# Between two layers of a decoder trunk: four output tiles on all tokens, the next chunks split earlier, squares summed in narrow groups

## The chip, the cores and the metric

The kernel runs on one NeuronCore of a Trainium2 chip. The metric is the device time of one execution in microseconds (us). Three runs of the kernel before took 1275.55, 1278.9 and 1277.45 us; their median is 1277.45.

## The reference

Two layers work on 512 tokens of 1024 features in float32. Each layer has a token mixer and a gated feed-forward part, and each of these four sub-layers starts with a norm that is scaled and shifted by a condition:

```
h = rms_norm(x, norm_mix[i]) * (1.0 + sc1) + sh1
mix = stick_breaking_attention(h, ...) if i % 2 == 0 else dsa_attention(h, ...)   # both end in  o @ w_out
x = x + g1 * mix
h = rms_norm(x, norm_ffn[i]) * (1.0 + sc2) + sh2
x = x + g2 * conv_ffn(h, ...)                                                     # ends in  (silu(gate) * val) @ w_down
```

where `rms_norm(x, g)` is `x * rsqrt(mean(x * x) + 1e-6) * g`, the mean over the 1024 features of a token.

## The kernel before

Everything lies transposed: features on the 128 partitions, tokens along the free side. `x` is eight tiles of 128 features x 512 tokens, and stays on the chip.

**Products.** A float32 product is made of three matmuls in a rounded float format (`mm3`, L247): high part of the weights times high part of the activations, low times high, high times low. A weight chunk is 128 x 1024 numbers (512 KB). `chunk_raw` (L175) loads it into one of six buffers in turn (`raws`); ScalarE copies it into its high part (`split_hi`, L208), VectorE subtracts to get the low part (`split_lo`, L216). High and low parts have four buffers each (`splits`), also taken in turn, so a split waits until the matmuls of the chunk four places earlier are done. `split_order` lists all chunks in their order of use, `pos` is the next one to split, and `fetch` issues loads, one chunk ahead of the split. All loads go through SyncE's queue (SP) in order; each waits only until the buffer that it fills has been read.

**Order of the work.** The order on each engine is the order of the program; every engine works through its own instructions strictly in that order and waits on semaphores for the others.

**Boundaries.** `boundary` (L376) joins a sub-layer that ends in an output projection to the next one, which starts with a norm and projections. It is called three times: at the end of the first attention (at about 241 us), of the first feed-forward part (609 us) and of the second attention (882 us). The very end of the kernel has a function of its own (`final_proj`, L476). In a boundary the last four weight chunks (`last`) give eight output tiles of 128 features. Before the change each is made in two halves of 256 tokens, `halves[0]` and `halves[1]`, each with 4 x 3 matmuls into a PSUM tile (`pt_l`). The steps of one tile are:

- `add_to_x` (L359, VectorE) adds the tile, times a gate, to `x`;
- `square` (L285, ScalarE) squares the new `x` into `sqt`;
- for the first half, `square_add` (L293, VectorE) adds the squares of tiles 0 to 6 into `sqa`;
- `sum_squares` (L298, TensorE) sums over the partitions by a float32 matmul with a matrix of ones: two of them for the first half, eight (one for each tile) for the second.

Then `norm_seed` (L315, ScalarE) takes a reciprocal square root, `norm_newton` (L321 to L323, VectorE) refines it, and `norm_ops` makes h, feature tile by feature tile: `u` (L330, VectorE), the high part of h (L333, ScalarE), its low part (L339, VectorE). The norm of the first half runs beside the output tiles of the second half, all of its steps ahead of the next projections. The next projections (`pt_first`) run first on the first half, four of them, and then, in `second_half`, on the second half. The four chunks that they need (`first`) are split during the second half's output tiles (two) and at the start of the next projections (two). ScalarE loads the function table of the reciprocal square root (`warm`, L374) after output tile 4.

PSUM has eight banks; a tile of the ring "z" or "tr" (two banks each) is free again when `add_to_x` has read it.

**Around it.** In the first attention `out_steps` (L827) runs the projection of the first half of the heads as filler, and `release` behind each of its four chunks splits the next chunk. In the second attention `uvc` (value weights) uses the buffers of the squares, which are idle then.

## Time and profile before

| | |
|---|---|
| median of three runs | 1277.45 us |
| profiled execution | 1276.47 us |
| its span (first to last instruction) | 1274.7 us |
| TensorE busy | 1263.3 us, 99% |
| VectorE busy | 926.8 us, 73% |
| ScalarE busy | 585.7 us, 46% |
| granted TensorE clock | 1.00 of full speed in all slices |

A page of the profile comes from one execution. In it PE is TensorE's matmuls, PEld its weight loads (which overlap the matmuls), DVE is VectorE, ACT ScalarE, POOL GpSimd, SP SyncE. Matmuls are pipelined: the duration of one holds more than its share of the engine, so the distance from one start to the next is what it costs. The same holds, less strongly, for VectorE and ScalarE.

### The profile page before, as it was taken

Reading aid. Unit: us, or ns where it says so; the run is one execution under the profiler, and the core shown is the slowest. Engines: PE = TensorE matmul, PEld = TensorE weight load, DVE = VectorE, ACT = ScalarE, POOL = GpSimd, SP = SyncE. Lnnn points to the kernel's source line nnn. Section 1 sums busy time; section 2 is a strip of 40 time slices with the busy share of each in tenths; the row PEclk is TensorE's granted clock in tenths of the full one; section 3 lists DMA queues with packets and bytes.
Section 4 is the critical chain, followed back from the end, with each engine's and each line's share of the span. In section 5 each row is a group of like instructions: output and inputs, shape, how many; then the busy total and the mean of one; then the engine's idle time right before and its main releaser. Section 6 shows DMA issues by size and latency. Waiting matters only on the chain.

```text
span 1274.7 us, 17853 instructions
## 1 busy us (share of the span) xinstructions
PE 1263.3 (99%) x6800; PEld 1055.8 (83%) x6800; DVE 926.8 (73%) x1587; ACT 585.7 (46%) x1041; POOL 60.5 (5%) x171
## 2 busy tenths in 40 slices
PE   8999999999999999999999999999999999999998
PEld 6888787898888888888987777888988888888887
DVE  5889998778777877885768878887866456456653
ACT  5477666454323323442445446655554334234430
POOL 0000000000000000000002350110000000000000
PEclk9999999999999999999999999999999999999999
DMA  9644444424575575655222222123232432423221
GB/s 369 216 137 133 136 130 135 130 67 122 197 254 185 179 242 193 188 182 159 85 67 67 84 75 74 52 83 115 68 88 69 125 95 73 127 85 99 75 91 67
DMA packets 49605, 163.15 MB, mean 128 GB/s; under 512 B 5696, under 2 KB 6720, under 8 KB 49520
## 3 DMA queue, kind: packets, MB, share of 16 engines
q1 hardware_dynamic: 49088, 161.23, 40.2%
q8 instruction: 53, 0.87, 0.3%
q10 hardware_dynamic: 432, 0.79, 0.2%
q14 instruction: 32, 0.26, 0.1%
HBM read 159.86 MB, written 2.14 MB: 127 GB/s over the span
## 4 chain that ended last, share of the span: by engine, by line
PE 93%; DVE 4%; DMA 1%; ACT 1%; issue 1%; SPq 0%; DVEq 0%
PE pt_u L248 11%; PE pt_u L249 11%; PE pt_u L250 11%; PE pt_d L248 5%; PE pt_d L249 5%; PE pt_d L250 5%; PE pt_l L249 2%; PE pt_l L250 2%; PE pt_l L248 2%; PE pt_first L249 2%; PE pt_first L248 2%; PE pt_first L250 2%; PE pt_q L248 2%; PE pt_q L250 2%; PE pt_q L249 2%; PE pt_qk L248 1%
## 5 line engine op out<-in xcount | busy, mean ns | idle before, releaser
L208 ACT ACTIVATE whi<-raw 128x1024 fp32r<-128x1024 f32 (+1 forms) x206 | 205.2, 1003 | 123.7 <-PE pt_d L250 95.5
L248 PE MATMUL pt_u<-hhi,whi 128*128 128x512 f32 x640 | 249.2, 389 | 0.0
L249 PE MATMUL pt_u<-hhi,wlo 128*128 128x512 f32 x640 | 249.0, 389 | 0.0
L250 PE MATMUL pt_u<-hlo,whi 128*128 128x512 f32 x640 | 249.0, 389 | 0.0
L216 DVE TENSOR_TENSOR wlo<-raw,whi 128x1024 fp32r<-128x1024 f32 (+1 forms) x194 | 223.5, 1154 | 11.6 <-ACT whi L208 10.6
L995 ACT ACTIVATE y<-pt_u,sm 128x512 f32<-128x512 f32 x80 | 62.2, 777 | 188.3 <-PE pt_u L250 188.3
L248 PEld LDWEIGHTS pt_u<-hhi,whi 128*128 128x128 f32 x640 | 120.1, 188 | 26.0 <-issue 1.1
L250 PEld LDWEIGHTS pt_u<-hlo,whi 128*128 128x128 f32 x640 | 120.1, 188 | 25.1
L249 PEld LDWEIGHTS pt_u<-hhi,wlo 128*128 128x128 f32 x640 | 120.1, 188 | 24.6
L996 DVE SCALAR_TENSOR_TENSOR y<-pt_u,sm,y 128x511 f32<-128x511 f32 x80 | 59.9, 748 | 97.1 <-ACT y L995 96.9
L248 PE MATMUL pt_d<-acthi,whi 128*128 128x512 f32 x288 | 112.0, 389 | 0.0
L249 PE MATMUL pt_d<-acthi,wlo 128*128 128x512 f32 x288 | 112.0, 389 | 0.0
L250 PE MATMUL pt_d<-actlo,whi 128*128 128x512 f32 x288 | 112.0, 389 | 0.0
L257 DVE SCALAR_TENSOR_TENSOR raw<-raw,cond 128x1024 f32<-128x1024 f32 x88 | 106.5, 1216 | 3.8 <-DMA raw<-wst 2.7
L359 DVE SCALAR_TENSOR_TENSOR x<-pt_d,mod,x 128x512 f32<-128x512 f32 x48 | 36.0, 749 | 72.8 <-PE pt_d L250 72.8
L232 ACT ACTIVATE acthi<-y 128x512 fp32r<-128x512 f32 x44 | 27.8, 632 | 105.3 <-DVE y L1014 105.3
L248 PE MATMUL pt_first<-hhi,whi 128*128 128x256 f32 (+1 forms) x224 | 68.5, 306 | 0.0
L249 PE MATMUL pt_first<-hhi,wlo 128*128 128x256 f32 (+1 forms) x224 | 67.1, 300 | 0.8 <-DVE wlo L216 0.8
L250 PE MATMUL pt_first<-hlo,whi 128*128 128x256 f32 (+1 forms) x224 | 66.9, 299 | 0.0
L250 PEld LDWEIGHTS pt_d<-actlo,whi 128*128 128x128 f32 x288 | 54.1, 188 | 11.3
L248 PEld LDWEIGHTS pt_d<-acthi,whi 128*128 128x128 f32 x288 | 54.1, 188 | 11.2
L249 PEld LDWEIGHTS pt_d<-acthi,wlo 128*128 128x128 f32 x288 | 54.1, 188 | 11.1
(253 smaller groups left out, 2594.8 us busy)
## 6 DMA issues: line engine op xcount, KB each, us to landing
raw<-wst SPq DMA_DIRECT2D x250, 512.0 KB, 3.7
raw<-wst SPq DMA_DIRECT2D x48, 384.0 KB, 3.1
th<-rb SPq DMA_DIRECT2D x16, 256.0 KB, 3.2
ada<-wst SPq DMA_DIRECT2D x4, 512.0 KB, 6.8
outT<-x SPq DMA_DIRECT2D x7, 256.0 KB, 2.0
x<-xT SPq DMA_DIRECT2D x5, 256.0 KB, 6.3
x<-xT ACTq DMA_DIRECT2D x3, 256.0 KB, 3.8
cond<-crow SPq DMA_DIRECT2D x1, 512.0 KB, 9.4
```

The lines of the kernel that those rows point to most:

```text
L208: act.activation(hi[:, :n], raw[:, :n], AF.Copy)
L216: engine.tensor_sub(lo[:, :n], raw[:, :n], hi[:, :n].bitcast(F32))
L232: act.activation(hi, src, AF.Copy)
L248: pe.matmul(out, lhsT=whi, rhs=ahi, start=start, stop=False)
L249: pe.matmul(out, lhsT=wlo, rhs=ahi, start=False, stop=False)
L250: pe.matmul(out, lhsT=whi, rhs=alo, start=False, stop=stop)
L257: dve.scalar_tensor_tensor(raw, raw, 1.0, cond, op0=OP.mult, op1=OP.mult, accum_out=dst)
L359: dve.scalar_tensor_tensor(x[f][:, c], pt, mod[l][:, g * KT + f:g * KT + f + 1], x[f][:, c], op0=OP.mult, op1=OP.add)
L995: act.activation(y, pt, AF.Identity, scale=cw[2], bias=sm[:, b + S_CB + c:b + S_CB + c + 1])
L996: dve.scalar_tensor_tensor(y[:, 1:], pt[:, :S - 1], cw[1], y[:, 1:], op0=OP.mult, op1=OP.add)
```

## The change

The first four output tiles of a boundary are made on all 512 tokens at once, the other four in halves as before. Their squares are also taken on all tokens, and `square_add` sums tiles 0 to 3 for both halves (tile 0 is squared straight into `sqa`). For the second half there remain five tiles of squares: the sum of tiles 0 to 3, and tiles 4 to 7. The first four of these five go through `group_squares`: four matmuls with 32 columns of the ones matrix, each writing its own 32 partitions of one PSUM tile; `copy_groups` (ScalarE) copies that tile, and two full matmuls then sum the copy and tile 7. This happens between the k steps of the next projections.

The last two of the four chunks of the output projection are split at the start of the boundary into spare buffers (`spare_tile`): attention buffers that are idle by then, or a pair of their own in the feed-forward part. For that, `release` falls away behind the last two chunks in `out_steps`. The table is loaded right after these splits. The four chunks of the next projections are split beside tiles 0 to 3. The norm steps of the first half are spread: five of its ten steps come ahead of the next projections, the others between their k steps. `norm_newton`'s temporary shares the buffers of `u`, and the value weights come in two loads instead of four.

```diff
+    whole = slice(0, S)
+
+    def square(f, c):
+        if f == 0:
+            sqs["acc"] = npool.tile([P, S], F32, name="sqa")
+            act.activation(sqs["acc"], x[f], AF.Square)
+            return None
+        if f < 4 or f % 2 == 0:
+            sqs["t"] = npool.tile([P, S], F32, name="sqt", bufs=2)
+        t = sqs["t"][:, :] if f < 4 else sqs["t"][:, halves[f % 2]]
+        act.activation(t, x[f][:, c], AF.Square)
         return t
 
-    def square_add(f, t):
-        if f == 0:
-            a = sqs["acc"] = npool.tile([P, H2], F32, name="sqa")
-            dve.tensor_copy(a, t)
-        else:
-            dve.tensor_add(sqs["acc"], sqs["acc"], t)
-
-    def sum_squares(t, start, stop):
-        if start:
-            sqs["pt"] = ptile([P, H2], "pt_norm", "z")
-        pe.matmul(sqs["pt"], lhsT=ones_mean, rhs=t, start=start, stop=stop)
+    def square_add(t, c):
+        if t is not None:
+            dve.tensor_add(sqs["acc"][:, c], sqs["acc"][:, c], t)
+
+    def sum_squares(tiles):
+        sqs["pt"] = ptile([P, H2], "pt_norm", "z")
+        for i, t in enumerate(tiles):
+            pe.matmul(sqs["pt"], lhsT=ones_mean, rhs=t, start=i == 0, stop=i == len(tiles) - 1)
+
+    def group_squares(tiles):
+        sqs["q"] = ptile([P, H2], "pt_sq", "x")
+        for i, t in enumerate(tiles):
+            pe.matmul(sqs["q"][32 * i:32 * i + 32], lhsT=ones_mean[:, :32], rhs=t, start=True, stop=True)
+
+    def copy_groups():
+
+        g = sqs["acc"][:, halves[0]]
+        act.activation(g, sqs["q"], AF.Copy, scale=D / 32)
+        return g
 
...
-        t = npool.tile([P, H2], F32, name="nt")
+        t = npool.tile([P, H2], F32, name="nt", tag="u", bufs=4)
...
-    def boundary(last, O, l, gate, nxt, first):
-
+    def boundary(last, O, l, gate, nxt, first, spare_tile):
 
         cks = [chunk(k, 0) for k in last[:2]]
-        unsplit = lambda: pos["i"] <= order.index(last[3])
         nl, gcol, sh, sc = nxt
         new_h()
         norm_scale(nl, gcol, sc)
-        while unsplit():
-            split_hi()
-            split_lo()
+        for i in range(2):
+            split_hi(lambda name, i=i: spare_tile(i, name))
+            split_lo(lambda name, i=i: spare_tile(i, name))
         cks += [chunk(k, 0) for k in last[2:]]
         fetch(pos["i"] + 1)
+        warm(AF.Abs_reciprocal_sqrt)
 
         begun = {}
 
-        def out_steps(hf, m, ks):
-            c = halves[hf]
+        def out_steps(c, m, ks):
             whi, wlo = cks[m // 2]
             if m not in begun:
-                begun[m] = ptile([P, H2], "pt_l", "tr" if hf or m % 2 == 0 else "z")
+                begun[m] = ptile([P, c.stop - c.start], "pt_l", "z" if m % 2 else "tr")
             for k in ks:
                 w = k * 256 + (m % 2) * P
                 mm3(begun[m], whi[:, w:w + P], wlo[:, w:w + P], O[k][0][:, c], O[k][1][:, c], k == 0, k == 3)
 
-        def out_tile(hf, m):
-
-            if hf or m > 2:
-                out_steps(hf, m, range(4))
-            elif m == 0:
-                for ks in (range(3), range(3, 4)):
-                    for i in range(3):
-                        out_steps(hf, i, ks)
-            add_to_x(l, gate, m, begun.pop(m), halves[hf])
-            return square(m, hf)
+        def out_done(c, m):
+            add_to_x(l, gate, m, begun.pop(m), c)
+            return square(m, c)
 
         prev = None
         for m in range(KT):
-            t = out_tile(0, m)
-            if prev is not None:
-                square_add(m - 1, prev)
+            c = whole if m < 4 else halves[0]
+            if m == 0:
+                for ks in (range(3), range(3, 4)):
+                    for i in range(2):
+                        out_steps(c, i, ks)
+            elif m > 1:
+                out_steps(c, m, range(4))
+            split_lo()
+            if m < 4:
+                split_hi()
+            t = out_done(c, m)
+            square_add(prev, whole if m < 5 else halves[0])
             prev = t
+        ops0 = norm_ops(nl, sh, 0)
+        group = [sqs["acc"][:, halves[1]]]
+        for m in range(4, KT):
+            c = halves[1]
             if m == 4:
-                warm(AF.Abs_reciprocal_sqrt)
-        ops0 = norm_ops(nl, sh, 0)
-        pend = []
-        for m in range(KT):
-            if m == 1:
-                sum_squares(sqs["acc"], True, False)
-                sum_squares(prev, False, True)
+                out_steps(c, m, range(3))
+                sum_squares([sqs["acc"][:, halves[0]], prev])
                 norm_seed(0)
-            if m >= 3:
-                sum_squares(pend[m - 3], m == 3, False)
-            pend.append(out_tile(1, m))
-            if m == 1:
+                out_steps(c, m, range(3, 4))
                 norm_newton(0)
-            if m in (2, 4):
-                split_hi()
-            if m in (3, 5):
-                split_lo()
-            for _ in range((0, 0, 1, 1, 2, 1, 2, 2)[m]):
-                next(ops0, None)
-        for m in range(KT - 3, KT - 1):
-            sum_squares(pend[m], False, False)
-        for _ in ops0:
-            pass
-        pts = [ptile([P, S], "pt_first", "mm" if i < 3 else "x") for i in range(4)]
+                next(ops0)
+            else:
+                out_steps(c, m, range(4))
+            if m == KT - 1:
+                next(ops0)
+            group.append(out_done(c, m))
+            if m < KT - 1:
+                next(ops0)
+        pts = [ptile([P, S], "pt_first", "mm") for i in range(3)]
         cs = [chunk(k, 0) for k in first[:2]]
-        split_hi()
         hs, c = hcur["h"], halves[0]
         for k in range(KT):
             for i in range(2):
                 w = slice(k * P, (k + 1) * P)
                 mm3(pts[i][:, c], cs[i][0][:, w], cs[i][1][:, w], hs[k][0][:, c], hs[k][1][:, c], k == 0, k == KT - 1)
-            if k == 1:
-                sum_squares(pend[KT - 1], False, True)
+            if k == 0:
+                group_squares(group[:4])
+                quarters = copy_groups()
+            if k == 2:
+                sum_squares([quarters, group[4]])
                 norm_seed(1)
-                split_lo()
+            next(ops0, None)
+            if k == 4:
                 norm_newton(1)
-                split_hi()
         ops1 = norm_ops(nl, sh, 1)
         for i in range(2, 4):
             for _ in range(2):
                 next(ops1, None)
             cs.append(chunk(first[i], 0))
+            if i == 3:
+                pts.append(ptile([P, S], "pt_first", "x"))
             project(pts[i][:, c], cs[i], hs, c)
         for _ in ops1:
             pass
...
-                    release()
+                    if mp < 2:
+                        release()
 
...
+                             lambda i, name: ap.tile([P, LW], F32R, name=name, tag=("at", "a")[i])[:, :D])
...
-                                [("kw",), ("qi", 0), ("qi", 1), ("qi", 2)]), man
+                                [("kw",), ("qi", 0), ("qi", 1), ("qi", 2)],
+                                lambda i, name: fp.tile([P, D], F32R, name=name, tag="spare" + name, bufs=2)), man
...
-                uvc = [npool.tile([P, H2], F32, name="uvc", tag="sqt" if i < 3 else "sqa", bufs=3 if i < 3 else 1) for i in range(4)]
-                for i in range(4):
-                    nc.sync.dma_start(uvc[i], wst[CH["uv",], :, i * H2:(i + 1) * H2])
+                uvc = [npool.tile([P, S], F32, name="uvc", tag="sqt", bufs=2) for i in range(2)]
+                for i in range(2):
+                    nc.sync.dma_start(uvc[i], wst[CH["uv",], :, i * S:(i + 1) * S])
...
-                first = boundary([("do", 1, m) for m in range(4)], O[4:], l, 2, (l, S_NF, 3, 4), up_first(l))
+                first = boundary([("do", 1, m) for m in range(4)], O[4:], l, 2, (l, S_NF, 3, 4), up_first(l),
+                                 lambda i, name: ap.tile([P, LW], F32R, name=name, tag=("L", "pT")[i], bufs=2)[:, :D])
```

## Rows read from the trace of the kernel before

**Rows 1.** The page: the span, the busy time of each engine, the engines' shares of the chain that ended last, and the loads of weight chunks (count, size, median us from issue to landing).
```profile
span 1274.7 us, 17853 instructions
PE 1263.3 (99%) x6800; PEld 1055.8 (83%) x6800; DVE 926.8 (73%) x1587; ACT 585.7 (46%) x1041; POOL 60.5 (5%) x171
...
PE 93%; DVE 4%; DMA 1%; ACT 1%; issue 1%; SPq 0%; DVEq 0%
...
raw<-wst SPq DMA_DIRECT2D x250, 512.0 KB, 3.7
```

**Rows 2.** Busy time by stage: the sum over the first boundary from its first output matmul at 241.15 to 279.90 us (taken in three stretches; the means are over these), and the start of the third boundary. Columns of the second row: from:to, length, then busy us and instructions of each engine, granted clock of TensorE, share of the DMA engines, GB/s.
```profile
sum 38.75, PE 38.75 PEld 38.22 DVE 30.64 ACT 21.23 POOL 0.00; mean PE 12.92 PEld 12.74 DVE 10.21 ACT 7.08 POOL 0.00
...
882.20:895.30 13.10, 12.15 (x101) 11.95 (x100) 10.10 (x21) 6.80 (x12) 0.00 (x0) 1.00 0.37 120
```

**Rows 3.** The chain that ended last, in order of time (start, us, what): in the first boundary the first and the last of 107 output matmuls of 256 columns in a row, the two sums behind them and one later sum; and the first and the last of 14 matmuls of 512 columns in a feed-forward part.
```profile
241.53 0.12 PE pt_l L249
...
254.25 0.12 PE pt_l L250
254.37 0.86 PE pt_norm L298 x4
...
258.09 0.43 PE pt_norm L298 x2
...
399.94 0.23 PE pt_u L250
...
402.89 0.23 PE pt_u L248
```

**Rows 4.** TensorE's matmuls in order of time (start, us, instruction) around a group of narrow sums in the second attention: four matmuls of 32 output partitions and 512 columns, each in two passes; one matmul between 706.33 and 707.19 is left out.
```profile
705.54 0.39 PE L250 MATMUL pt_q<-hlo,whi 128*128 128x512 f32 x1
705.86 0.63 PE L1117 MATMUL ssg<-q2g,ones_mean 128*32 128x512 f32 x3
705.88 0.62 PE L1117 MATMUL ssg<-q,ones_mean 128*32 128x512 f32 x1
706.31 0.60 PE L1117 MATMUL ssg<-q2g,ones_mean 128*32 128x512 f32 x3
706.33 0.59 PE L1117 MATMUL ssg<-q,ones_mean 128*32 128x512 f32 x1
...
707.19 0.39 PE L249 MATMUL pt_q<-hhi,wlo 128*128 128x512 f32 x1
```

**Rows 5.** The start of the third boundary in order of time, all engines; in brackets the idle time of the engine before the instruction and what ended it.
```profile
883.14 0.63 ACT L1483 ACTIVATE ohi<-bs 128x512 fp32r<-128x512 f32 x1 [1.59 <-DVE bs L1480]
883.81 0.69 DVE L1487 TENSOR_TENSOR olo<-bs,ohi 128x512 fp32r<-128x512 f32 x1 [0.70 <-ACT ohi L1483]
884.42 1.22 DVE L216 TENSOR_TENSOR wlo<-raw,whi 128x1024 fp32r<-128x1024 f32 x1
884.46 0.28 PE L248 MATMUL pt_l<-ohi,whi 128*128 128x256 f32 x1
885.69 0.39 PE L249 MATMUL pt_l<-ohi,wlo 128*128 128x256 f32 x1 [0.95 <-DVE wlo L216]
885.91 0.28 PE L250 MATMUL pt_l<-olo,whi 128*128 128x256 f32 x1
```

**Rows 6.** VectorE and ScalarE in order of time, each line the start and the length of one instruction: an add of 512 columns and the low part behind it (second boundary); then, in the first boundary, a squares' add of 256 columns, the table load, the seed, the three steps behind it and what follows them, a u and a low part of h, a high part of a chunk, a low part of a chunk and what follows it.
```profile
604.89 0.75 DVE L359 SCALAR_TENSOR_TENSOR x<-pt_d,mod,x 128x512 f32<-128x512 f32 x1 [2.20 <-PE pt_d L250]
605.55 1.22 DVE L216 TENSOR_TENSOR wlo<-raw,whi 128x1024 fp32r<-128x1024 f32 x1
...
253.37 0.42 DVE L293 TENSOR_TENSOR sqa<-sqa,sqt 128x256 f32<-128x256 f32 x1
...
249.66 1.28 ACT L374 ACT_TABLE_LOAD   x1
255.31 0.46 ACT L315 ACTIVATE ln<-pt_norm,ecols 128x256 f32<-128x256 f32 x1
257.10 0.41 DVE L321 TENSOR_TENSOR nt<-ln 128x256 f32<-128x256 f32 x1
...
258.35 0.48 DVE L359 SCALAR_TENSOR_TENSOR x<-pt_l,mod,x 128x256 f32<-128x256 f32 x1
262.30 0.47 DVE L330 SCALAR_TENSOR_TENSOR u<-ln,sfac,x 128x256 f32<-128x256 f32 x1
262.70 0.48 DVE L339 SCALAR_TENSOR_TENSOR hlo<-u,mod,hhi 128x256 fp32r<-128x256 f32 x1
262.75 1.04 ACT L208 ACTIVATE whi<-raw 128x1024 fp32r<-128x1024 f32 x1
264.28 1.21 DVE L216 TENSOR_TENSOR wlo<-raw,whi 128x1024 fp32r<-128x1024 f32 x1
265.41 0.47 DVE L330 SCALAR_TENSOR_TENSOR u<-ln,sfac,x 128x256 f32<-128x256 f32 x1
```

**Rows 7.** The loads at the first boundary: two low parts on VectorE (start, length), SyncE's queue of loads (the first of five starts at 235.73, the last ends 26.22 later, most of it waiting), and the loads issued from 230 to 245 us (count, size, median us from issue to landing).
```profile
234.49 1.21 DVE L216 TENSOR_TENSOR wlo<-raw,whi 128x1024 fp32r<-128x1024 f32 x1
242.86 1.22 DVE L216 TENSOR_TENSOR wlo<-raw,whi 128x1024 fp32r<-128x1024 f32 x1 [0.25 <-ACT whi L208]
235.73 26.22 SPq L177 DMA_DIRECT2D raw<-wst  x5
raw<-wst SPq DMA_DIRECT2D x5, 512.0 KB, 4.4
```

More of the change, by code (lines that the diff above doesn't have):

```diff
@@ L281, in kernel_body @@
     sqs = {}
-    def square(f, hf):
-        t = npool.tile([P, H2], F32, name="sqt", bufs=3)
-        act.activation(t, x[f][:, halves[hf]], AF.Square)
-        return t
-    def square_add(f, t):
-        if f == 0:
-            a = sqs["acc"] = npool.tile([P, H2], F32, name="sqa")
-            dve.tensor_copy(a, t)
-        else:
-            dve.tensor_add(sqs["acc"], sqs["acc"], t)
-    def sum_squares(t, start, stop):
-        if start:
-            sqs["pt"] = ptile([P, H2], "pt_norm", "z")
-        pe.matmul(sqs["pt"], lhsT=ones_mean, rhs=t, start=start, stop=stop)
+    whole = slice(0, S)
[8 more added lines that the diff above has]
+        act.activation(t, x[f][:, c], AF.Square)
+        return t
+    def square_add(t, c):
[13 more added lines that the diff above has]
+        return g
     hcur = {}
@@ L490, in done @@
             nc.sync.dma_start(outT[m][:, c], x[m][:, c])
-        whole = slice(0, S)
         for m in range(2):
@@ L977, in stick_layer @@
             first = boundary([("o", 1, m) for m in range(4)], [O[4 + k] for k in range(4)], l, 2,
-                             (l, S_NF, 3, 4), up_first(l))
+                             (l, S_NF, 3, 4), up_first(l),
+                             lambda i, name: ap.tile([P, LW], F32R, name=name, tag=("at", "a")[i])[:, :D])
         return first, man
@@ L1443, in pair_values @@
                         pe.matmul(pv[:, k * P:(k + 1) * P], lhsT=latf[:, k * P:(k + 1) * P],
-                                  rhs=uvc[h // 4][:, h % 4 * 64:h % 4 * 64 + P], start=True, stop=True)
+                                  rhs=uvc[h // 8][:, h % 8 * 64:h % 8 * 64 + P], start=True, stop=True)
                     vals[h] = [npool.tile([P, H2], F32, name="vals", tag="u", bufs=4) for _ in range(2)]
```

## The prediction, made before the changed kernel was run

> **What bounds the kernel now.** I read the page first, then the stages around the three boundaries, then single instructions. The reader is to see on the page that TensorE is busy 99% of the span at the full granted clock, and that it makes up 93% of the chain that ended last [rows 1]. So time goes only where TensorE gets less work or where one of its few gaps closes. The table of stages shows no gap in the first boundary: TensorE is busy for all of the 38.75 us, while VectorE has 30.64 us of work and ScalarE 21.23 [rows 2]. The third boundary has one: 12.15 us of work in 13.10 [rows 2]. The change must therefore be judged by TensorE's work first, and then by whether VectorE and ScalarE still deliver in time.
>
> **Part 1: four tiles on all tokens.** In the chain, the 256-column output matmuls run from 241.53 to the start of the squares at 254.37, 107 of them, so 0.1200 us each [rows 3]. The 512-column ones go from 399.94 to 402.89 in 13 steps, 0.2269 us each [rows 3]. One wide one thus saves 2 x 0.1200 - 0.2269 = 0.0131 us. Tiles 0 to 3 hold 4 x 12 = 48 such pairs in a boundary: 0.63 us, and 1.9 us in three boundaries.
>
> **Part 2: the sums of squares.** Before, a boundary has two of them for the first half of the tokens and eight for the second. The chain gives 0.86 us for two and 0.43 for one [rows 3], so ten cost 4.30 us. After it, two full ones for the first half stay (0.86), then four narrow ones that write 32 partitions each, then two full ones (0.86). The trace has the narrow form with 512 columns: from the start of the matmul ahead of it (705.54) to the second one behind it (707.19) are 1.65 us, of which two wide matmuls take 0.45; the group costs 1.20 [rows 4]. Its two passes start 0.45 us apart, side by side over all four (705.86 to 705.88, then 706.31 to 706.33), so the columns account for some 0.85 and the rest, 0.34, is paid around it. With 256 columns I estimate 0.43 + 0.34 = 0.77 us. From both sides: 0.43 (nothing around it) and 4 x 0.43 = 1.72 (no overlap). I take 0.77, since the row is the same form. A boundary then pays 0.86 + 0.77 + 0.86 = 2.49, saves 1.81, and three save 5.4 us. The Trainium skill, "TensorEngine Tiling (Array Packing)", section "Tiling Modes", speaks against the narrow form: a change of tiling mode drains the engine. The 0.34 us of the row agree with it. The same page, section "Overview", gives up to four times the speed for outputs of at most 32; by that alone the group would cost 0.43 and the sum would be 1.0 us lower.
>
> **Part 3: the gap at the third boundary.** TensorE starts a matmul at 884.46 and the next at 885.69, released by a low part, and the one after that follows at 0.22 instead of 0.12: 1.11 + 0.10 = 1.2 us lost [rows 5]. It is tile 2, which needs the second chunk's low part; VectorE began that only at 884.42, behind the last head's. With two tiles on all tokens ahead, TensorE has 18 x 0.2269 = 4.1 us for k = 0 to 2 and 1.4 for k = 3, so tile 2 starts near 887.7, when that low part (done 885.55) has been there for 2 us. The k = 3 operand, begun at 883.81 and 0.69 long [rows 5], is asked for at 886.4. The gap goes, and I see none that takes its place: -1.2 us.
>
> **Part 4: what moves on VectorE and ScalarE.** The four splits of the next chunks come into the first part, one to each wide tile. VectorE's prices, start to start: 0.66 for an add of 512 columns, 1.13 for a low part [rows 6]; for the squares' add of 512 columns, which the trace lacks, 0.42 to 0.69, by its 256-column form below and by a subtraction of 512 columns above (0.69 long, the next 0.61 after it) [rows 5, 6]; I take 0.61. A tile costs 0.66 + 0.61 + 1.13 = 2.40 us of VectorE against 12 x 0.2269 = 2.72 of TensorE. ScalarE needs 1.04 for a high part and, by a copy of 512 columns, some 0.63 for a square [rows 5, 6]. Both fit. The last low part falls beside tile 4, where TensorE takes 1.44 and VectorE 2.14; tiles 5 to 7 bring 0.40 + 0.42 against 1.44 each and take that up. The table load of 1.28 us [rows 6] moves from tile 4 to the start, where ScalarE waits for the first tile anyway: nothing, and 1.3 us of ScalarE if that cover were gone.
>
> The first half's norm loses its slack. Count from the end of its two sums: the seed needs 0.6 (0.46 long), the three steps behind it 1.25 (257.10 to 258.35), then VectorE does three u, two output adds and the first low part at 0.40 each, the last 0.48 long, so the first low part is there after some 4.4 us [rows 6]. TensorE asks for it after 0.36 + 3 x 1.44 + 0.24 = 4.9. That is 0.5 us to spare. Later k need 0.80 us of VectorE against 0.72 of TensorE, but gain the group's 0.77 and the sum's 0.86. The copy of the group is queued behind the last square, which waits for the last add: about 9.5 us after tile 4 of the second half began, and TensorE asks for it at 9.55. I add 0.1 us for each boundary. The second half's norm starts near 11.9 and ends near 19.7 on the same count, while TensorE reaches its last operand after 22.
>
> In the first boundary the loads are the narrow place. Six buffers take the raw chunks in turn. Before, the load that waits starts at 235.73, when the low part at 234.49 is done [rows 7]. That chunk is now split inside the boundary, so the buffer comes free at about 244.0 (the other engine work ahead of it is as in the row at 242.86) and the second new chunk lands 3.7 to 4.4 us later, 247.7 to 248.4 [rows 1, 7]. Its high part would start at 246.7 on ScalarE, so it and the squares behind it wait. VectorE's queue from that low part on to the last squares' add (three low parts, two adds and three squares' adds of 512 columns, four and three of 256) gives 9.4 us; the sums are due near 258.9, so the low part must start by 249.5 and the chunk land by 248.5. I put 0.2 us on this. The loads of the other two boundaries find buffers that were free earlier, and cost nothing. The wider square tiles, the two loads instead of four of the value weights, and the temporary that shares a ring with u I cost at nothing: their users are long done.
>
> **Sum.** -1.9 - 5.4 - 1.2 + 3 x 0.1 + 0.2 = -8.0 us. The profiled execution took 1276.47 us, 1.77 more than its span, and lies 0.98 under the median of the three runs, 1277.45. So 1268.5 for an execution like it, and 1269.4 as a median.
>
> **Rivals.**
> The late chunk. If the second new chunk of the first boundary lands 3 us later than I count, TensorE waits about that long once: 1272.4. For it: four loads come free at once, and the median landing in that stretch is already 4.4 us [rows 7]; against it: the chunk is first in its queue.
> The group does not overlap. Then it costs 1.72, 0.95 more in each boundary: 1272.3. Against it stand the pairs of starts 0.02 us apart in the narrow rows [rows 4].
> The gain is eaten in part by norms. If the first low part is 2.5 us late in each boundary, TensorE loses 2.0 each: 6 of the 8 us go, 1275.4, no change. For it: half of the norm steps now stand behind the start of the next projection; against it: the prices are measured on the same instructions.
> Slower. The same chain from 3.2 us late on, that is when three low parts of 1.13 us are still queued ahead of the seed's steps in all three boundaries: every further us costs three, and 4.2 us late would give 1280.5. For it: VectorE has only 0.3 us of slack on a wide tile and is strictly in order; against it: tiles 5 to 7 give back 1.9 us, and VectorE sheds two low parts and eight half-width adds from the stretches behind.
> That the change doesn't do what it says: the wide tiles and the group are plain instruction counts, so I see no room for that.
>
> **Chances.** The forecast 0.65, the late chunk 0.12, no overlap 0.05, norms that eat it 0.10, slower 0.08. The first three are all faster by over 0.3% (3.8 us, about what a measurement of this kernel can tell): 0.82. Within 0.3%: 0.10, slower by more: 0.08. The range runs from 1266.4 (the group at 0.43, no new waits, and a run 1.5 us under the median, as the lowest one shown is 1.9 under) to 1274.0 (both milder rivals and the start of the third): about 0.8.
>
> **What would show it.** Output matmuls of 512 columns at 0.227 apart and 144 fewer of them in all three boundaries together; a group of narrow matmuls of about 0.8 us; eight sums instead of ten; no wait of TensorE for a low part near 885; a first sum that starts 1.1 us behind tile 7; next to no idle time of TensorE before the next projection's matmuls. Wrong: idle time there that is released by a low part of h or by the copied group, or VectorE still on chunk splits when the seed's steps are due.

## The result, and the profile after

Six runs of the changed kernel gave a median of 1268.84 us (1268.12 to 1272.04), six of the kernel before 1277.59 us (1275.55 to 1280.61). The ratio is 0.9941, with a 95% interval of 0.9929 to 0.9952: faster, by 0.5 to 0.7%. The forecast was 1269.4.

The time by stage is worked out from the starts of TensorE's matmuls. A boundary runs here from its first `pt_l` matmul to the start of its last `pt_first` matmul; the stages between are what is left.

| us | up to B1 | B1 | feed-forward 1 | B2 | attention 2 | B3 | feed-forward 2 |
|---|---|---|---|---|---|---|---|
| before | 240.11 | 50.23 | 317.39 | 50.19 | 223.25 | 51.49 | 337.74 |
| after | 239.66 | 48.49 | 317.39 | 48.19 | 226.44 | 48.23 | 337.74 |

The boundaries became 1.74, 2.00 and 3.26 us shorter, 7.00 in all. The page of after first, with the parts that answer to [rows 1], then busy time by stretch: most of the first boundary, the start of the third [rows 2], and the one stretch in which this execution lost time. Columns as in [rows 2]; the granted clock is the number behind POOL's.

```profile
span 1270.3 us, 17505 instructions
PE 1260.6 (99%) x6644; PEld 1045.5 (82%) x6644; DVE 926.3 (73%) x1572; ACT 584.9 (46%) x1032; POOL 57.9 (5%) x171
...
PE 93%; DVE 4%; DMA 1%; ACT 1%; issue 1%; SPq 0%; DVEq 0%
```

```profile
240.76:279.50 38.74, 38.74 (x271) 35.62 (x272) 32.14 (x65) 22.22 (x40) 0.00 (x0) 1.00 0.27 85
...
757.80:764.60 6.80, 5.03 (x31) 3.97 (x30) 6.21 (x16) 4.21 (x12) 0.47 (x1) 1.00 0.28 71
...
764.60:771.40 6.80, 6.80 (x26) 6.11 (x26) 3.80 (x11) 2.07 (x8) 0.00 (x0) 0.50 0.09 20
...
882.00:895.30 13.30, 13.30 (x72) 11.51 (x71) 12.57 (x17) 10.46 (x13) 0.00 (x0) 1.00 0.65 212
```

Three readings. TensorE has 156 matmuls fewer, 6644 for 6800: 144 by the wide tiles, and three times two sums of two passes. The third boundary's gap of [rows 2] is gone: 13.30 us busy of 13.30. And the attention ahead of it is 3.2 us longer in this execution: from 764.6 to 771.4 TensorE had a granted clock of 0.50, its level of 1.2 GHz instead of 2.4, after it had been busy for only 5.03 of 6.80 us. Nothing ties that to the change. TensorE waits there in the same three places (0.34 to 0.39, 0.66 to 0.68 and 0.71 to 0.72 us) in all 14 profiled executions of this document, the kernel before included; behind them the clock fell in 7, one of them of the kernel before with a low part moved, and in the other 7 it did not. The same kernel with one sum moved (below) had 223.25 us there, at 1.00 throughout. It accounts for what this profiled execution, 1272.04 us, lies above the median.

Inside the first boundary, the chain that ended last in order of time (start, us, what), as in [rows 3]: the 4th and the 48th wide matmul, the first half's pair of sums, the narrow group, the second pair.

```profile
241.66 0.23 PE pt_l L248
...
251.92 0.23 PE pt_l L250
...
258.97 0.97 PE pt_norm L303 x4
...
265.32 0.58 PE pt_sq L308 x8
...
267.52 1.07 PE pt_norm L303 x4
```

Forty-four steps in 10.26 us are 0.233 us each, not the 0.227 of [rows 3]. Both pairs of sums take longer than the 0.86 of [rows 3]. The group itself, in TensorE's order of time (the two lines with x3 hold three matmuls each):

```profile
265.04 0.28 PE L250 MATMUL pt_first<-hlo,whi 128*128 128x256 f32 x1
265.25 0.40 PE L308 MATMUL pt_sq<-sqa,ones_mean 128*32 128x256 f32 x1
265.25 0.43 PE L308 MATMUL pt_sq<-sqt,ones_mean 128*32 128x256 f32 x3
265.49 0.38 PE L308 MATMUL pt_sq<-sqa,ones_mean 128*32 128x256 f32 x1
265.50 0.40 PE L308 MATMUL pt_sq<-sqt,ones_mean 128*32 128x256 f32 x3
265.83 0.39 PE L248 MATMUL pt_first<-hhi,whi 128*128 128x256 f32 x1
266.05 0.28 PE L249 MATMUL pt_first<-hhi,wlo 128*128 128x256 f32 x1
```

Four matmuls start together, and their second passes 0.24 us later. From 265.04 to 266.05 are 1.01 us; less two ordinary steps of 0.12 the group costs 0.77, the price that the prediction estimated from the 512-column form [rows 4].

Where the rest went is seen in VectorE, ScalarE and TensorE together (the lines are put in order of time from the views of the engines):

```profile
246.68 0.63 ACT L288 ACTIVATE sqa<-x 128x512 f32<-128x512 f32 x1 [0.89 <-DVE x L375]
247.22 1.04 ACT L208 ACTIVATE whi<-raw 128x1024 fp32r<-128x1024 f32 x1
...
258.34 0.42 DVE L298 TENSOR_TENSOR sqa<-sqa,sqt 128x256 f32<-128x256 f32 x1
258.81 0.30 PEld L303 LDWEIGHTS pt_norm<-sqa,ones_mean 128*128 128x128 f32 x2
258.81 0.69 PE L303 MATMUL pt_norm<-sqa,ones_mean 128*128 128x256 f32 x2
...
263.84 0.48 DVE L355 SCALAR_TENSOR_TENSOR hlo<-u,mod,hhi 128x256 fp32r<-128x256 f32 x1
264.24 0.47 DVE L375 SCALAR_TENSOR_TENSOR x<-pt_l,mod,x 128x256 f32<-128x256 f32 x1
264.68 0.28 PE L250 MATMUL pt_first<-hlo,whi 128*128 128x256 f32 x1
265.03 0.48 DVE L355 SCALAR_TENSOR_TENSOR hlo<-u,mod,hhi 128x256 fp32r<-128x256 f32 x1
...
266.72 0.42 ACT L293 ACTIVATE sqt<-x 128x256 f32<-128x256 f32 x1 [0.28 <-DVE x L375]
267.05 0.36 ACT L313 ACTIVATE sqa<-pt_sq 128x256 f32<-128x256 f32 x1
267.47 0.70 PE L303 MATMUL pt_norm<-sqa,ones_mean 128*128 128x256 f32 x2
```

The last squares' add ends at 258.76 and the sum starts at 258.81, its weights loaded in the same moment and not ahead: the pair costs 0.96 instead of 0.86, so 0.1 us. The second pair starts at 267.47, behind the copy of the group (to 267.41), which stands behind the last square on ScalarE: 0.1 us for the late start and 0.1 for its weights, 0.21 in all. In the second boundary the start is later, and the two make 0.33; in the third it is 0.21 again. The first low part of h is there at 264.32, and TensorE uses it at 264.68: 0.36 us to spare. The second new chunk's high part starts at 247.22 right behind a square, with no idle time: no load is late.

### The profile page after: what moved, and what is told of

Read it like the earlier page. It is cut to its first block, busy times and chain, and to the rows that moved or that the text cites. A ratio compares the mean times of both kernels' runs of the same rounds, so it can differ in the third digit from the quotient of the medians.

```text
span 1270.3 us, 17505 instructions
## 1 busy us (share of the span) xinstructions
PE 1260.6 (99%) x6644; PEld 1045.5 (82%) x6644; DVE 926.3 (73%) x1572; ACT 584.9 (46%) x1032; POOL 57.9 (5%) x171
## 4 chain that ended last, share of the span: by engine, by line
PE 93%; DVE 4%; DMA 1%; ACT 1%; issue 1%; SPq 0%; DVEq 0%
PE pt_u L248 11%; PE pt_u L250 11%; PE pt_u L249 11%; PE pt_d L248 5%; PE pt_d L250 5%; PE pt_d L249 5%; PE pt_l L248 2%; PE pt_first L248 2%; PE pt_q L248 2%; PE pt_first L249 2%; PE pt_l L250 2%; PE pt_l L249 2%; PE pt_first L250 2%; PE pt_q L250 2%; PE pt_q L249 2%; PE pt_qk L248 1%
```

## The experiments

All times stand beside runs of the kernel before on the same chip.

**The changed kernel again**, with no edit.

> The changed kernel once more, for a profile without the stretch at half clock. Theory (the gain is TensorE's work and one gap, all inside the three boundaries): from the first output matmul to the last matmul of the next projections the boundaries take 48.5, 48.2 and 48.2 us again (before: 50.2, 50.2, 51.5), the second attention 223.3 us as before, and the span is 1267. Rival (something outside the boundaries pays too): another stage is shorter by 0.5 us or more.

1269.26 us (1268.48 to 1271.51), ratio 0.9945 (0.9933 to 0.9958); boundaries of 48.49, 48.19 and 48.24 us. It gave no profile without the stretch at half the clock: the second attention took 226.44 us again, and the span was 1269.7 us, not 1267. The boundaries repeat to 0.01 us, so they can be compared much more closely than whole executions. The stage ahead of the first boundary does not repeat like that: 239.11 us here, 239.66 above.

**Full sums in place of the narrow group.**

```diff
-            if k == 0:
-                group_squares(group[:4])
-                quarters = copy_groups()
             if k == 2:
-                sum_squares([quarters, group[4]])
+                sum_squares(group)
```

> The changed kernel with five full sums in place of the narrow group, its copy and two full sums. Theory (the four narrow sums run side by side for 0.77 us): five full ones cost 5 x 0.43 = 2.15 against 0.77 + 2 x 0.43 = 1.63, and the wait for the copy (0.1 to 0.3) goes, so each boundary is 0.2 to 0.5 us longer, 1.1 us in all. Rival (no overlap, the group costs 1.72): each boundary is 0.4 us shorter, 1.3 us in all.

1270.73 us, ratio 0.9957 (0.9943 to 0.997); boundaries 49.14, 48.85 and 48.89, so 0.65 us longer each, more than the 0.2 to 0.5 of the theory. By the prices five sums for a group and two are 2.15 - 0.77 - 0.86 = 0.52. The rest is on balance waits for low parts of h (in the first boundary steps of 0.275, 0.223 and 0.201 instead of 0.12), less the wait at the second pair, which is gone: the group had given VectorE 0.77 us in which to make these low parts. The group overlaps and pays.

**The kernel before, with one low part ahead of the last head's work.**

```diff
+                split_lo()
                 weighted(HEADS - 2)
                 pair_hi()
```

> The kernel before with one thing moved: VectorE makes the waiting low part of the weights before the last head's work, not behind it, at the third boundary. Theory (TensorE's gap there is that low part's place in VectorE's queue): the gap of 1.2 us goes, the third boundary takes 50.3 us in place of 51.5, the time is 1.2 us lower. Rival (the gap belongs to the last head's own operand): nothing moves, or the operand comes 0.3 us later and the gap stays.

B3 fell from 51.49 to 50.30 us, 1.19 less; 1276.12 us, ratio 0.9993 (0.9984 to 1.0001), too little to show in the whole. The start of the third boundary, to be set against [rows 2]:

```profile
882.20:895.30 13.10, 13.10 (x112) 12.61 (x109) 10.43 (x22) 7.00 (x13) 0.00 (x0) 1.00 0.39 121
```

So the gap was the order on VectorE, as read from [rows 5], and is worth what was forecast.

**The second pair of sums one product later.**

```diff
-            if k == 2:
+            if k == 3:
                 sum_squares([quarters, group[4]])
```

> The changed kernel with the second half's two last sums one k step later (behind k = 3, not k = 2). Theory (TensorE waits 0.1 to 0.3 us there for the copied group): each boundary is 0.1 to 0.3 us shorter, 0.5 us in all. Rival (the second half's norm has no slack): the next projections on the second half wait for it, 0.7 us longer in each boundary.

Boundaries 48.31, 48.02 and 48.05: 0.18, 0.17 and 0.18 less. 1269.28 us, ratio 0.9945 (0.9933 to 0.9958), the same as the changed kernel as far as whole runs tell. The pair costs 0.86 now, so the wait at it is real and was not priced high enough; some 0.04 us of it come back as a wait at a later step.

**The splits of the next chunks back among the second half's tiles.**

```diff
-            split_lo()
-            if m < 4:
-                split_hi()
             t = out_done(c, m)
...
             group.append(out_done(c, m))
+            if m in (4, 6):
+                split_hi()
+            if m in (5, 7):
+                split_lo()
...
         cs = [chunk(k, 0) for k in first[:2]]
+        split_hi()
...
+            if k == 1:
+                split_lo()
             next(ops0, None)
             if k == 4:
                 norm_newton(1)
+                split_hi()
```

> The changed kernel with the four splits of the next chunks put back among the second half of the tokens and the steps of the norm (two high parts behind tiles 4 and 6, two low parts behind 5 and 7, the rest of them at the first products of the next projection). My theory: the norm chain on VectorE has about 0.5 us to spare for the first low part of h, so low parts of 1.13 us that stand ahead of the norm steps or among them make TensorE wait: some 1 to 2.5 us in each boundary, 1272 to 1276 us in all, with idle time of TensorE before the next projection's matmuls that ends with VectorE's low parts of h. Rival: where the splits stand makes no difference, 1269 us, boundaries within 0.2 us of the changed kernel's 48.49, 48.19 and 48.23.

1290.41 us (1288.77 to 1292.31), ratio 1.0105 (1.009 to 1.0121): slower than the kernel before, and the boundaries 56.11, 55.25 and 55.90, longer by 7.1 to 7.7 us where 1 to 2.5 were expected. TensorE at the start of the next projections of the first boundary, and two stretches there:

```profile
264.57 0.28 PE L248 MATMUL pt_first<-hhi,whi 128*128 128x256 f32 x1
265.64 0.38 PE L249 MATMUL pt_first<-hhi,wlo 128*128 128x256 f32 x1 [0.80 <-DVE wlo L216]
266.44 0.38 PE L250 MATMUL pt_first<-hlo,whi 128*128 128x256 f32 x1 [0.41 <-DVE hlo L355]
268.29 0.39 PE L248 MATMUL pt_first<-hhi,whi 128*128 128x256 f32 x1 [1.47 <-ACT whi L208]
269.94 0.58 PE L249 MATMUL pt_first<-hhi,wlo 128*128 128x256 f32 x1 [1.27 <-DVE wlo L216]
```

```profile
264.57:269.38 4.81, 1.43 (x6) 0.63 (x4) 4.81 (x10) 3.49 (x9) 0.00 (x0) 1.00 0.33 109
269.38:276.20 6.82, 6.26 (x27) 4.87 (x28) 4.41 (x9) 2.08 (x4) 0.00 (x0) 0.50 0.52 156
```

Two things add up. The splits stand in line behind high parts and adds that themselves wait, on two engines in turn: ScalarE for a u, VectorE for a high part, TensorE for both. The five steps from 264.57 to 270.3 lost 5.15 us against 0.12 each. The granted clock fell to 0.50 from 269.4 to 276.2, after 1.43 us of work in 4.81, and the matmuls there start 0.213 us apart instead of 0.12, which makes up most of the remaining 2.5. The place of the splits carries more than the whole change gives.

**Five raw buffers instead of six.**

```diff
-    raws = ctx.enter_context(tc.tile_pool(name="raws", bufs=6))
+    raws = ctx.enter_context(tc.tile_pool(name="raws", bufs=5))
```

> The changed kernel with five buffers for the raw chunks instead of six, so that in each boundary a chunk's load must wait for a split more. Theory of the late chunk: in the first boundary the load then waits for a low part that ends near 243.5 us and lands near 247.2 or later, when ScalarE wants it at 244.8; the work behind it on VectorE is 9.4 us, so the first sum comes 0.6 to 1.0 us late and this boundary grows from 48.49 to 49.1 to 49.5 us; the two others change by less than 0.2; 1269.5 to 1270 us. Rival: the splits have more slack than I count, the first boundary stays within 0.2 us of 48.49 and the time at 1269.

Boundaries 48.49, 48.19 and 48.22, unchanged to 0.01 us; 1270.95 us (1268.19 to 1273.28), ratio 0.9952 (0.9939 to 0.9965), which overlaps that of the changed kernel. No load is late, even with a buffer less.

**One sum in the first half.**

```diff
-                out_steps(c, m, range(3))
-                sum_squares([sqs["acc"][:, halves[0]], prev])
+                square_add(prev, halves[0])
+                out_steps(c, m, range(4))
+                sum_squares([sqs["acc"][:, halves[0]]])
...
-            if k == 2:
+            if k == 3:
```

> The changed kernel with the squares of the first half's tile 7 added by VectorE too, so that the first half needs one full sum instead of two, placed behind all four steps of tile 4 of the second half, and the second half's last pair of sums behind the fourth product of the next projection instead of the third. Theory: a full sum less (0.43) and no wait at the two places (0.2 to 0.3) make each boundary 0.6 to 0.75 us shorter than the changed kernel's 48.49, 48.19 and 48.23: about 2 us in all, near 1267 us. Rival: VectorE's extra add (0.42) and the later sum use up the norm chain's 0.5 us, and TensorE waits 0.3 to 0.7 us for the first low parts of h: the boundaries then stay within 0.3 us.

Boundaries 48.45, 48.13 and 48.20, no more than 0.06 less; 1270.66 us, ratio 0.9948 (0.9936 to 0.9961). The one sum costs 0.75 us and not 0.43, since TensorE waits for it, so that part is 0.21 us shorter; the second pair, a product later, is 0.2 us shorter too. The projections give it back: 0.1 to 0.15 us at the first low parts, and the group, which is now reached before ScalarE has squared the last of its tiles (at 267.04), takes 1.0 us instead of 0.77; the rest are smaller waits:

```profile
266.62 0.42 ACT L293 ACTIVATE sqt<-x 128x256 f32<-128x256 f32 x1 [0.34 <-DVE x L375]
266.64 0.29 PE L250 MATMUL pt_first<-hlo,whi 128*128 128x256 f32 x1
...
266.87 0.63 PE L308 MATMUL pt_sq<-sqt,ones_mean 128*32 128x256 f32 x3
...
267.86 0.28 PE L249 MATMUL pt_first<-hhi,wlo 128*128 128x256 f32 x1
```

**One sum in each half.** The first half as above; in the second half:

```diff
             if k == 0:
-                group_squares(group[:4])
+                square_add(group[1], halves[1])
+            if k == 2:
+                group_squares([group[0]] + group[2:])
                 quarters = copy_groups()
-            if k == 2:
-                sum_squares([quarters, group[4]])
+            if k == 4:
+                sum_squares([quarters])
                 norm_seed(1)
             next(ops0, None)
-            if k == 4:
+            if k == 5:
                 norm_newton(1)
```

> As the kernel with one sum in the first half, and in the second half VectorE adds tile 4's squares to the accumulator, the narrow group takes the accumulator and tiles 5 to 7, and one full sum of the copied group is left, behind the fifth product, the second norm a product later. Theory: another full sum less, so 1.0 to 1.2 us less in each boundary than the changed kernel, about 3.2 us in all, near 1266 us. Rival: the added add stands ahead of the first half's norm steps on VectorE or the second half's norm comes late, and TensorE waits for it at the low parts of h: no better than the kernel with one sum in the first half alone.

Boundaries 48.46, 48.15 and 48.22; 1270.7 us, ratio 0.9953 (0.994 to 0.9965). The rival held: TensorE waits some 0.4 us at the second low part of h (steps of 0.49 to 0.54 us).

**One sum in the first half, the group one product later.**

```diff
-            if k == 0:
+            if k == 1:
                 group_squares(group[:4])
...
-            if k == 2:
+            if k == 4:
                 sum_squares([quarters, group[4]])
...
-            if k == 4:
+            if k == 5:
                 norm_newton(1)
```

(with the edit of the first half as in the kernel with one sum there)

> One sum in the first half (VectorE adds tile 7's squares as well, the sum behind all four steps of tile 4), the narrow group behind the second product of the next projection instead of the first, the last pair of sums behind the fifth and the second norm's steps behind the sixth. The kernel with one sum lost its gain again at the group, which TensorE reached before the last squares were there (1.0 us for it instead of 0.77). Theory: one product later the squares are there, so the group costs 0.77 again, the pair of sums does not wait, and each boundary ends 0.5 to 0.7 us below the changed kernel's 48.49, 48.19 and 48.23, near 1267.5 us in all. Rival: VectorE's norm chain is the bound, TensorE waits at the second low part of h instead, and the boundaries stay within 0.3 us.

A miss: boundaries 48.68, 48.34 and 48.41, 0.15 to 0.19 longer than the changed kernel's. 1268.84 us (1268.74 to 1272.6), ratio 0.9943 (0.993 to 0.9956). The group is back at 0.77, but the wait has moved to the second low part, and VectorE is busy for 4.96 of 5.00 us around it:

```profile
266.97 0.38 PE L250 MATMUL pt_first<-hlo,whi 128*128 128x256 f32 x1 [0.22 <-DVE hlo L355]
...
263.00:268.00 5.00, 4.78 (x43) 4.14 (x41) 4.96 (x13) 3.44 (x8) 0.00 (x0) 1.00 0.00 0
```

**One low part later, at two places** (N is 6 in the first kernel and 7 in the second).

```diff
-            split_lo()
             if m < 4:
+                split_lo()
                 split_hi()
...
             group.append(out_done(c, m))
+            if m == N:
+                split_lo()
```

> The changed kernel with one thing put later: the last of the four low parts of the next chunks stands behind VectorE's output add of tile 6 of the second half, among the norm steps. By the rows of the changed kernel it then runs from some 264.6 to 265.9 us in the first boundary, and TensorE asks for it at 264.97: theory (VectorE's order in the norm stretch sets the time) 0.8 to 1.1 us more in each boundary, about 3 us in all, near 1272 us, at the full granted clock, since the wait is short. Rival: the norm chain has slack enough and the boundaries stay within 0.3 us; second rival: the wait brings TensorE to its lower clock as in the kernel with all splits late, and each boundary loses 3 us or more.

> The same low part one tile later still, behind the output add of tile 7: it then ends near 267.8 us in the first boundary, where TensorE asks for it at 264.97. Theory: TensorE waits 2.8 us in each boundary; if its clock stays up, the boundaries grow by 2.5 to 3 us each (1277 us in all, the whole gain given back); if the wait brings it to the lower level (1.2 GHz, granted clock 0.5), as in the kernel with all splits late, by up to 3.4 us more each (to 1287 us). Which of the two it is, the granted clock of the stretch behind the wait shows.

Behind tile 6: boundaries 49.63, 49.37 and 49.36, so 1.13 to 1.18 us more each; 1272.37 us, ratio 0.9961 (0.9948 to 0.9975). Behind tile 7: 48.74, 48.44 and 48.47, only 0.25 more; 1270.71 us, ratio 0.9951 (0.9938 to 0.9963). Both expectations went wrong on one premise: this is the low part of the fourth chunk, and TensorE doesn't ask for it at 264.97 but only in the fourth projection. That the first came out near its 0.8 to 1.1 us is in part luck. What the two show is the other thing, the room in VectorE's line. The first kernel, VectorE and TensorE in order of time:

```profile
264.64 1.22 DVE L216 TENSOR_TENSOR wlo<-raw,whi 128x1024 fp32r<-128x1024 f32 x1
...
266.17 0.48 DVE L355 SCALAR_TENSOR_TENSOR hlo<-u,mod,hhi 128x256 fp32r<-128x256 f32 x1
266.70 0.38 PE L250 MATMUL pt_first<-hlo,whi 128*128 128x256 f32 x1 [0.36 <-DVE hlo L355]
...
268.61 0.70 PE L303 MATMUL pt_norm<-sqa,ones_mean 128*128 128x256 f32 x2 [0.38 <-ACT sqa L313]
```

The second low part of h starts at 266.17 instead of 265.03, and TensorE loses the whole 1.14 us: 0.52 at that low part, 0.44 at the copied group, whose last square waits for an add behind it, the rest in weights not loaded ahead. In the second kernel the low part of the weights starts two low parts of h and an add later, and costs 0.25:

```profile
266.98 1.21 DVE L216 TENSOR_TENSOR wlo<-raw,whi 128x1024 fp32r<-128x1024 f32 x1
```

The granted clock stayed at 1.00 in both boundaries.

**The table load back behind tile 4.**

```diff
-        warm(AF.Abs_reciprocal_sqrt)
...
             prev = t
+            if m == 4:
+                warm(AF.Abs_reciprocal_sqrt)
```

> The changed kernel with the load of ScalarE's function table put back behind tile 4 of the first half. ScalarE then spends 1.28 us there, where it is busy with the squares of tiles 4 to 7. Theory: squares of 0.42 to 0.63 us each 1.44 us leave it room to catch up before the last square, so the boundaries change by 0 to 0.1 us and the time not at all. Rival: the last squares come 0.5 us or more late and with them the sum and the norm: 0.5 to 1.3 us more in each boundary, up to 1273 us.

B1 and B2 unchanged (48.49 and 48.19), B3 48.71, which is 0.48 longer; 1270.95 us, ratio 0.9947 (0.9935 to 0.9959). Neither side had it: the place matters in one boundary of three. The third boundary:

```profile
893.70 1.28 ACT L390 ACT_TABLE_LOAD   x1
...
895.11 0.71 ACT L293 ACTIVATE sqt<-x 128x256 f32<-128x256 f32 x2
895.88 0.48 DVE L375 SCALAR_TENSOR_TENSOR x<-pt_l,mod,x 128x256 f32<-128x256 f32 x1
896.28 0.42 DVE L298 TENSOR_TENSOR sqa<-sqa,sqt 128x256 f32<-128x256 f32 x1
```

The load holds two squares until 895.11, VectorE's line moves back with them, and TensorE's step to the first sum is 0.59 us, where it is 0.12 in the changed kernel.

## Why the prediction was right, point by point

The direction, the terms and the result held; the time agrees better than the terms do. The terms made 8.0 us, the three boundaries gave 7.0, and the two medians differ by 8.75. What lies between these is not shown to be the change: the stage ahead of the first boundary took from 239.1 to 241.3 us in the profiled executions (240.11 in the kernel before, 239.44 in the same kernel with a low part moved in another stage), and some have the stretch at half the clock. In the second comparison, of 15 runs and 5, the medians were 1276.65 and 1269.26, which differ by 7.4. So that 1269.4 came so near to 1268.84 is partly luck: the boundaries gained 1.0 us less than forecast, and the first comparison shows 1.75 more than they gained.

| term | forecast, three boundaries | measured |
|---|---|---|
| Part 1, wide tiles | -1.9 | -1.5 |
| Part 2, sums without waits | -5.4 | -5.4 (group 0.77, a sum 0.43) |
| Part 3, gap at the third boundary | -1.2 | -1.2 |
| Part 4, waits | +0.5 | +1.2 (what is left to 7.0) |

- **Part 1** was mis-sized. The 48 wide matmuls take 11.30, 10.88 and 11.03 us by their starts, against 11.63, 11.51 and 11.62 for the 96 of half the width (the third taken from the kernel with the gap closed). That saves 0.32, 0.63 and 0.59; no run has the wide tiles alone, so this is read from the starts. The second boundary has the forecast 0.63; in the first the wide ones stay 0.233 apart. I took the step of the feed-forward part for all three, where the trace of the kernel before already had the slower step: in the first attention, just ahead of that boundary, 75 steps of its 512-column projection matmuls have a mean of 0.232 us, and four starts in a row are

```profile
228.37 0.40 PE L250 MATMUL pt_o<-olo,whi 128*128 128x512 f32 x1
228.60 0.39 PE L248 MATMUL pt_o<-ohi,whi 128*128 128x512 f32 x1
228.83 0.40 PE L249 MATMUL pt_o<-ohi,wlo 128*128 128x512 f32 x1
229.07 0.39 PE L250 MATMUL pt_o<-olo,whi 128*128 128x512 f32 x1
```

- **Part 2** held. The group of four costs 0.77, a pair of sums 0.86 where it doesn't wait, and without the group the boundaries are 0.65 longer. The two rules that were weighed come out as they did on [rows 4]: the Trainium skill, "TensorEngine Tiling (Array Packing)", section "Tiling Modes", has a change of mode drain the engine, and what is paid around the 0.43 us that were estimated for the columns is 0.34 here too. The factor of four of its section "Overview" alone, 0.43 for the group, is not reached.
- **Part 3** held: 1.19 us when that low part alone was moved in the kernel before; and the third boundary gained 1.26 more than the second.
- **Part 4** was mis-sized, and wrong in its place. "I add 0.1 us for each boundary" for the copied group became 0.21, 0.33 and 0.21, and the first half's pair, for which I had no wait, has 0.1 in each, since its last squares arrive just then. These make 1.05 of the 1.2; by what is left over in each boundary it is 0.39, 0.44 and 0.34. The 0.2 us for a late chunk was for nothing: the chunk is there when ScalarE gets to it.
- **"That is 0.5 us to spare"** for the first low part was nearly right: 0.36. The prediction didn't say what this slack does next. VectorE is full from there on, so TensorE's later savings end in waits: three kernels that save another full sum or two gain at most 0.06 us in a boundary or lose up to 0.19.
- **The table load**, costed at nothing, hides as said in two boundaries. That it moves ahead is worth 0.48 us in the third, where it would have stood in the way.
- **The slower rival** did not come about in the changed kernel. Its mechanism, low parts ahead of the norm's steps, is real: the old order of the splits, which puts them among these steps, made 1290.4 us. What I expected of that kernel, 1 to 2.5 us in each boundary, was too low twice over: like the rival's price it counted only VectorE's own time, where the splits also wait for ScalarE, and it left out that TensorE's clock fell behind these waits, for most of another 2.5 us in each boundary.
- **The range**'s upper end does not follow from what it names: both milder rivals on top of 1269.4 are 3.0 and 2.85 us, which makes 1275.2 and not 1274.0. Neither of them came.

No version beat the changed kernel by what whole runs can tell. Its second pair of sums one product later takes 0.53 us off the three boundaries, by the starts of the matmuls.

## What to carry to other kernels

When one engine is busy 99% of the time, count its instructions first; then ask which of its helpers becomes full where its work was cut, because that helper decides whether the next cut pays. Price a helper's instruction by its place in the line: the same 1.13 us on VectorE cost TensorE 1.14 us ahead of one low part and 0.25 two low parts later. And a moved preparation that looks like a side condition (here the splits) can be worth more than the edit that it makes room for.

## What the runs showed of the hardware

- Matmuls of 512 columns have two paces at the full granted clock: 0.227 us in the feed-forward parts and the second boundary, 0.229 and 0.237 in turn (0.233 in the mean) in all of the first boundary's, and in the third only for the first ten or so. Every kernel with the wide tiles showed it, and the 512-column projections of the first attention have it in the kernel before too (0.232 in the mean). The cause is open.
- Where a matmul's operand came just before it, its weights were loaded at the same moment instead of ahead (258.81 above): the step became 0.315 us instead of 0.215.
- The granted clock fell to 0.50 (1.2 GHz) behind stretches in which TensorE had waited, at each boundary with the old order of the splits and, in 7 of 14 profiled executions, in the second attention. Where it fell the wait was paid twice: once while it lasted, and once behind it, some 2.5 us in the one place and 1.5 or 3.2 in the other. In the second attention the same waits stand in the executions without a fall, so the waits alone do not tell whether it comes.
